# First part of an MLP: lower weight parts one K row behind the upper ones

## The chip, the cores and the metric

The kernel runs on one core of a Trainium2 chip. The metric is the device time of one execution in microseconds (us); the number given for a kernel is the median of several runs. TensorE (PE in the profile) multiplies, and its weight loads are shown as a row of their own (PEld). ScalarE (ACT), VectorE (DVE) and GpSimd (POOL) work on vectors, and SyncE (SP) issues the loads from memory.

## The reference

Two layers on 256 tokens of width 2048, everything in float32. Layer 0 mixes tokens with a convolution module, layer 1 with latent attention. Behind each of them comes an MLP with a hidden width of 8192:

```python
def sq_relu_mlp(h, w1, w2):
    return jnp.square(jax.nn.relu(h @ w1)) @ w2

for layer in range(DEPTH):
    h = rms_norm(x, norm_mixer_g[layer])
    x = x + (conv_module(h, ...) if layer % 2 == 0 else mla(h, ...))
    h = rms_norm(x, norm_mlp_g[layer])
    x = x + sq_relu_mlp(h, mlp_w1[layer], mlp_w2[layer])
return rms_norm(x, final_norm_g)
```

The change concerns the product `h @ w1`, in both layers.

## The kernel before

**Numbers in two parts.** A float32 value is split into an upper part (`hi`, rounded to the format float32r) and a lower part (`lo`, the remainder). A product of two such numbers is made of three: upper by upper, upper by lower, lower by upper. ScalarE makes the upper part of the weights (line 420) and VectorE the lower one (line 421).

**The up product.** The hidden width is cut into four parts (`q` = 0 to 3). Each part has eight pairs `p` of two tiles `b`, and a tile is 128 hidden columns for all 256 tokens. K, the width of 2048, is cut into 16 rows `k` of 128. The activations lie in `xt`: for each row `k` the upper parts of the 256 tokens and, beside them, the lower parts, so that `xhl(k)` is 512 columns wide and `xh(k)` its first 256. For each row TensorE loads the upper weight part and runs 512 columns (line 504), which gives two of the three products at once, and then loads the lower weight part and runs 256 columns (line 505). Both add into one PSUM tile of 512 columns. At the tile's end ScalarE copies it out (line 510), and VectorE adds its two halves (line 522).

**Units and chunks.** A tile's weights are a unit, one load of 1 MB. It is worked off in two chunks `h` of eight rows. A chunk's `prep` makes the two weight parts, in buffers of which there are six each (`WB`). Its `run` issues the matmuls. `stream` goes through the list of chunks and calls `prep` of up to five chunks ahead before `run` of the current one:

```python
while done[0] < min(n + (LOOK_UP if chunk.tight else WB), len(chunks)):
    ...
    prep()
...
chunk.run(parts[unit])
```

**Order.** The list begins with the 16 tiles of part 0, one directly after the other, and the first tile of part 1 follows them. From there on up tiles of part `q` + 1 stand singly between chunks of the down product of part `q`, which consist of 512-column matmuls (lines 195 to 197). Ahead of part 0, in both layers, stand the last transposes of the activations (line 251) that make `xt`; six of them lie inside its first tile. Each engine works off its instructions in the order in which they are written here, and semaphores keep the engines in step. A buffer is written again once the last reader of its earlier contents is through.

**What ties to the change.** The upper part of a chunk is last read by row 7 or 15 of line 504, the lower part by line 505 of the same row. The functions below are the ones that the change touches.

Of the kernel before, what the change touches and what calls it, by code (L numbers as in the profile page):

```python
# [20 lines left out]
KC = D // P  # L21
T = 2
S = T * P
# [59 lines left out]
def trunk_kernel(  # L83
# [26 lines left out]
    nc = tc.nc  # L110
# [28 lines left out]
    def nm(s):  # L139
        uid[0] += 1  # L140
        return f"{s}_{uid[0]}"


    def acc_tile():
        return psum["acc"].tile([P, NB], F32, tag="acc", name=nm("acc"))
# [41 lines left out]
    def rows(w, k0, nk, c0, n):  # L187

        return w[k0 * P : (k0 + nk) * P, c0 : c0 + n].rearrange(
            "(j p) n -> p j n", p=P  # L190
        )
# [128 lines left out]
    xh = lambda k: xhl(k)[:, :S]  # L320
# [95 lines left out]
    def hi_lo(n):  # L416
        return [wpool.tile([P, n, NB], F32R, tag=c, name=nm(c), bufs=WB) for c in ("hi", "lo")]

    def split_into(parts, src):
        nc.scalar.activation(parts[0], src, AF.Copy)  # L420
        nc.vector.tensor_tensor(parts[1], src, parts[0].bitcast(F32), op=ALU.subtract)  # L421
# [51 lines left out]
    def mlp(layer, ssq, next_gain, finish=None, before=None, last_w1=None):  # L473
# [5 lines left out]
        def u_tile():  # L479
            return first_tiles.pop("u", None) or mp.tile([P, 2, 2 * S], F32, tag="U", name=nm("U"), bufs=2)  # L480

        def f_tile():
            return first_tiles.pop("f", None) or mp.tile([P, 8, P], F32, tag="W", name=nm("W"), bufs=1)

        def up_units(hs, q, p, extra):

            sevens = SEVENS[layer][q]
            held = {}

            def up_unit(b):  # L490
                ps = []

                def chunk(h):
                    def prep(raw, parts):
                        parts[h] = [a.rearrange("p a (j n) -> p (a j) n", n=P) for a in hi_lo(2)]
                        split_into(parts[h], raw[:, 8 * h : 8 * h + 8, :])

                    def run(parts):
                        if not ps:
                            ps.append(acc_tile())  # L500
                        wh, wl = parts.pop(h)
                        for j in range(8):
                            k = 8 * h + j
                            nc.tensor.matmul(ps[0], wh[:, j, :], xhl(k), start=k == 0, stop=False)  # L504
                            nc.tensor.matmul(ps[0][:, :S], wl[:, j, :], xh(k), start=False, stop=k == KC - 1)  # L505

                    def out():
                        if b == 0:
                            held["u"] = u_tile()
                        nc.scalar.activation(held["u"][:, b, :], ps[0], AF.Copy)  # L510

                    if h == 0:
                        return Chunk(prep, run)
                    return Chunk(prep, run, [add, lambda: None, square, forms, part] + extra if b == 1 else [], now=out)

                unit = Unit(rows(w1, 0, KC, ((q * NPAIR + p) * 2 + b) * P, P), KC, [chunk(h) for h in range(2)])
                unit.last_read = 1
                return unit

            def add():  # L520
                v = held["u"][:, :, :S]
                nc.vector.tensor_tensor(v, v, held["u"][:, :, S:], op=ALU.add)

            def square():
                v = held["u"][:, :, :S]
                nc.scalar.activation(v, v, AF.Relu)
                if p in sevens:
                    held["f"] = f = f_tile()
                    nc.scalar.activation(f[:, 0:4, :].rearrange("p (b t) n -> p b (t n)", b=2), v, AF.Square)
                    held["src"], shape, tag, n = f[:, 1:8, :], [P, 7, P], "s", N_S  # L530
                else:
                    nc.scalar.activation(v, v, AF.Square)
                    held["src"], shape = v, [P, 2, S]
                    tag, n = ("s", N_S) if q == PARTS - 1 and p in LATE_G[layer] else ("g", N_G)
                held["hl"] = [mp.tile(shape, F32R, tag=tag + c, name=nm(tag + c), bufs=n) for c in "hl"]

            def forms():
                if p in sevens:
                    f = held["f"]
                    nc.vector.tensor_tensor(  # L540
                        f[:, 4:6, :], f[:, 0:1, :].broadcast_to([P, 2, P]), f[:, 1:3, :], op=ALU.subtract
                    )
                    nc.vector.tensor_tensor(f[:, 6, :], f[:, 1, :], f[:, 5, :], op=ALU.subtract)
                    nc.vector.tensor_tensor(f[:, 7, :], f[:, 3, :], f[:, 6, :], op=ALU.subtract)

            def part():
                hs[p] = held["hl"]
                split_into(hs[p], held["src"])

            return [up_unit(b) for b in range(2)]  # L550

        def down_units(hs, q, n2, held, final):
# [228 lines left out]
    with ExitStack() as cx:  # L781
# [40 lines left out]
        def conv_w(n, j):  # L822
            half = raws[n].shape[1] // 2
            hi, lo = wjs[n, j // half]
            return hi[:, j % half, :], lo[:, j % half, :]
# [174 lines left out]
        with tc.manual_schedule():  # L1000
# [143 lines left out]
            for m in range(NP):  # L1144
# [4 lines left out]
                for j in range(2):  # L1149
                    k = 2 * m + j  # L1150
                    wh, wl = conv_w(NU + m, j)
# [9 lines left out]
                t, i = divmod(m, NNB)  # L1161
# [68 lines left out]
    with ExitStack() as cx:  # L1230
# [73 lines left out]
        def w_at(key, j):  # L1304
            n = pieces[key]
            half = units[n][1][1] // 2
            hi, lo = parts[n, j // half]
            return hi[:, j % half, :], lo[:, j % half, :]
# [243 lines left out]
        with tc.manual_schedule():  # L1552
# [8 lines left out]
            ps = [[acc_tile() for _ in range(2)] for _ in range(T)]  # L1561
            for k in range(KC):
                u, j = divmod(k, 2)
# [6 lines left out]
                wh, wl = w_at(("kv", u), j)  # L1570
# [9 lines left out]
            ps = [acc_tile() for _ in range(T)]  # L1580
            for k in range(KC):
                u, j = divmod(k, 4)
# [3 lines left out]
                wh, wl = w_at(("q", u), j)  # L1586
# [176 lines left out]
```

## Time and profile before

| what | us |
|---|---|
| median of 3 runs | 1948.66 |
| lowest and highest run | 1948.26, 1950.67 |
| the profiled execution | 1952.0 |
| its span, first to last instruction | 1950.2 |
| TensorE busy in it | 1925.9 (99%) |

The granted TensorE clock was 0.999 of full speed over the span. Rows of the profile give a line of the kernel, an engine, an operation, the tile written and those read, the shape and a count; then busy time in us and the mean of one in ns. Rows of the timeline give the start and the duration in us. Matmuls overlap each other in these records, since each one's end is modelled with its way through the array: what one costs is the time from its start to the next start.

### The profile page before, as it was taken

The page shows a single profiled execution, that of the slowest core. Times are in us where ns is not written, and L with a number is a line of the kernel's source. Part 1 is how long each engine was busy: PE and PEld are TensorE (multiplying, and loading weights), DVE is VectorE, ACT ScalarE, POOL GpSimd, SP SyncE. Part 2 cuts the span into 40 slices and gives each one's busy share as a digit, 9 for nine tenths or more (in the row PEclk, how much of TensorE's full clock was granted, in tenths as well). Part 3 has the DMA queues.
Part 4 walks back from the last instruction along what each step waited for, and adds up shares of the span by engine and source line. Part 5 has one row for each costly group of instructions (what it writes and reads, how often), then busy time and mean ns, then how long its engine had stood idle before and what let it go on. Part 6 is the DMA issues. An engine that isn't in the chain of part 4 may idle for free.

```text
span 1950.2 us, 28404 instructions
## 1 busy us (share of the span) xinstructions
PE 1925.9 (99%) x10814; PEld 1681.3 (86%) x10814; DVE 1612.7 (83%) x2294; ACT 1196.1 (61%) x1695; POOL 223.8 (11%) x184
## 2 busy tenths in 40 slices
PE   7999999999999999999999999999999999999998
PEld 7999888888888888888899998888888888888886
DVE  5999866679998998898976665557999899889887
ACT  5556655666666666756566665566666566666644
POOL 5999300000000000000001410000000000000000
PEclk9999999999999999999999999999999999999999
DMA  8666356757666666766646445765666766666763
GB/s 237 181 180 188 131 193 183 207 154 216 192 206 197 202 194 202 216 185 213 200 149 181 118 148 175 213 174 169 196 196 205 206 205 195 191 207 197 226 205 108
DMA packets 407112, 367.61 MB, mean 188 GB/s; under 512 B 15416, under 2 KB 351936, under 8 KB 406720
## 3 DMA queue, kind: packets, MB, share of 16 engines
q1 hardware_dynamic: 405952, 363.63, 62.8%
q10 hardware_dynamic: 1024, 2.17, 0.3%
q8 instruction: 84, 1.38, 0.3%
q14 instruction: 52, 0.43, 0.1%
HBM read 363.68 MB, written 2.10 MB: 188 GB/s over the span
## 4 chain that ended last, share of the span: by engine, by line
PE 96%; ACT 1%; DVE 1%; DMA 1%; POOL 1%; issue 0%; DVEq 0%; ACTq 0%; POOLq 0%
PE acc L504 24%; PE acc L195 15%; PE acc L197 15%; PE acc L196 15%; PE acc L505 12%; PE acc L835 3%; PE acc L834 3%; PE acc L833 3%; PE acc L251 1%; PE sum L883 1%; PE acc L1531 0%; POOL lo L170 0%; DMA xs<-in_x 0%; ACT hi L169 0%; PE acc L1395 0%; PE acc L1396 0%
## 5 line engine op out<-in xcount | busy, mean ns | idle before, releaser
L504 PE MATMUL acc<-xt,hi 128*128 128x512 f32 x2048 | 718.6, 394 | 0.0
L421 DVE TENSOR_TENSOR lo<-raw,hi 128x1024 fp32r<-128x1024 f32 (+1 forms) x512 | 573.0, 1135 | 98.1 <-ACT hi L420 97.7
L505 PE MATMUL acc<-xt,lo 128*128 128x256 f32 x2048 | 574.4, 280 | 0.0
L420 ACT ACTIVATE hi<-raw 128x1024 fp32r<-128x1024 f32 (+1 forms) x512 | 491.0, 982 | 84.9 <-PE acc L196 68.5
L504 PEld LDWEIGHTS acc<-xt,hi 128*128 128x128 f32 x2048 | 384.4, 188 | 88.4
L505 PEld LDWEIGHTS acc<-xt,lo 128*128 128x128 f32 x2048 | 385.3, 188 | 3.7
L195 PE MATMUL acc<-hi,sh 128*128 128x512 f32 x814 | 319.4, 392 | 0.0
L197 PE MATMUL acc<-lo,sh 128*128 128x512 f32 x814 | 318.1, 391 | 0.0
L420 ACT ACTIVATE hi<-T 128x1024 fp32r<-128x1024 f32 x164 | 173.7, 1059 | 184.1 <-DVE T L696 124.8
L196 PE MATMUL acc<-hi,sl 128*128 128x512 f32 x686 | 267.3, 390 | 0.0
L421 DVE TENSOR_TENSOR lo<-T,hi 128x1024 fp32r<-128x1024 f32 x164 | 200.5, 1222 | 43.0 <-ACT hi L420 39.8
L169 ACT ACTIVATE hi<-raw 128x1024 fp32r<-128x1024 f32 (+2 forms) x184 | 179.9, 1005 | 44.9 <-PE acc L196 39.0
L170 DVE TENSOR_TENSOR lo<-raw,hi 128x1024 fp32r<-128x1024 f32 (+2 forms) x118 | 133.3, 1148 | 67.3 <-ACT hi L169 61.6
L510 ACT ACTIVATE U<-acc 128x512 f32<-128x512 f32 x128 | 76.1, 595 | 175.1 <-PE acc L505 175.0
L197 PEld LDWEIGHTS acc<-lo,sh 128*128 128x128 f32 x814 | 152.8, 188 | 33.6
L195 PEld LDWEIGHTS acc<-hi,sh 128*128 128x128 f32 x814 | 152.9, 188 | 32.4
L935 DVE SCALAR_TENSOR_TENSOR sum<-ub,w_dw,sum 128x256 f32<-128x256 f32 x400 | 162.7, 479 | 7.6 <-ACT sum L891 6.5
L170 POOL TENSOR_TENSOR lo<-raw,hi 128x1024 fp32r<-128x1024 f32 x66 | 157.7, 2412 | 24.4 <-ACT hi L169 24.4
L196 PEld LDWEIGHTS acc<-hi,sl 128*128 128x128 f32 x686 | 128.9, 188 | 24.0
L833 PE MATMUL acc<-xt,hi 128*128 128x256 f32 x512 | 145.3, 284 | 0.0
L834 PE MATMUL acc<-xt,hi 128*128 128x256 f32 x512 | 143.9, 281 | 0.4 <-DVE xt L208 0.4
L835 PE MATMUL acc<-xt,lo 128*128 128x256 f32 x512 | 144.0, 281 | 0.0
(265 smaller groups left out, 2756.4 us busy)
## 6 DMA issues: line engine op xcount, KB each, us to landing
raw<-in_mlp_w SPq DMA_DIRECT2D x256, 1024.0 KB, 6.1
raw<-in_conv_w_pw SPq DMA_DIRECT2D x64, 512.0 KB, 5.5
raw<-in_conv_w_pw SPq DMA_DIRECT2D x16, 1024.0 KB, 5.1
raw<-in_mla_w_o SPq DMA_DIRECT2D x16, 1024.0 KB, 5.8
raw<-in_mla_w_kv_up SPq DMA_DIRECT2D x8, 1024.0 KB, 5.6
raw<-in_mla_w_in SPq DMA_DIRECT2D x8, 576.0 KB, 3.8
raw<-in_mla_w_in SPq DMA_DIRECT2D x4, 1024.0 KB, 6.5
raw<-in_mla_w_q_up SPq DMA_DIRECT2D x16, 256.0 KB, 3.9
```

Source lines behind the costliest of these rows:

```text
L169: nc.scalar.activation(hi, raw[:, js, :], AF.Copy)
L170: eng.tensor_tensor(lo, raw[:, js, :], hi.bitcast(F32), op=ALU.subtract)
L195: nc.tensor.matmul(ps, sh, mh, start=start, stop=False)
L196: nc.tensor.matmul(ps, sl, mh, start=False, stop=False)
L197: nc.tensor.matmul(ps, sh, ml, start=False, stop=stop)
L420: nc.scalar.activation(parts[0], src, AF.Copy)
L421: nc.vector.tensor_tensor(parts[1], src, parts[0].bitcast(F32), op=ALU.subtract)
L504: nc.tensor.matmul(ps[0], wh[:, j, :], xhl(k), start=k == 0, stop=False)
L505: nc.tensor.matmul(ps[0][:, :S], wl[:, j, :], xh(k), start=False, stop=k == KC - 1)
L833: nc.tensor.matmul(o, wh[:, bs], xh(k), start=k == 0, stop=False)
L834: nc.tensor.matmul(o, wh[:, bs], xl(k), start=False, stop=False)
L835: nc.tensor.matmul(o, wl[:, bs], xh(k), start=False, stop=k == KC - 1)
```

## The change

In tiles of part 0 (`q == 0`) the matmul with the lower weight part of row `k` is issued after the matmul with the upper part of row `k` + 1. The sequence of a tile is hi0, hi1, lo0, hi2, lo1, and so on to hi15, lo14, lo15. The lower part of row 7, the last of the first chunk, is thus read in the second chunk's `run`, behind hi8. All other parts keep their order, since there `behind` is 0 and the list is emptied at once.

```diff
             def up_unit(b):
-                ps = []
+                ps, low, behind = [], [], int(q == 0)
...
                         for j in range(8):
                             k = 8 * h + j
                             nc.tensor.matmul(ps[0], wh[:, j, :], xhl(k), start=k == 0, stop=False)
-                            nc.tensor.matmul(ps[0][:, :S], wl[:, j, :], xh(k), start=False, stop=k == KC - 1)
+                            low.append((wl[:, j, :], k))
+                            while low and (len(low) > behind or k == KC - 1):
+                                a, i = low.pop(0)
+                                nc.tensor.matmul(ps[0][:, :S], a, xh(i), start=False, stop=i == KC - 1)
```

## The prediction

> **What bounds the kernel now.** I read the page first: the busy line, the chain and the two groups of the lines that change.
>
> ```profile
> span 1950.2 us, 28404 instructions
> ...
> PE 1925.9 (99%) x10814; PEld 1681.3 (86%) x10814; DVE 1612.7 (83%) x2294; ACT 1196.1 (61%) x1695; POOL 223.8 (11%) x184
> ...
> PE 96%; ACT 1%; DVE 1%; DMA 1%; POOL 1%; issue 0%; DVEq 0%; ACTq 0%; POOLq 0%
> ...
> L504 PE MATMUL acc<-xt,hi 128*128 128x512 f32 x2048 | 718.6, 394 | 0.0
> ...
> L505 PE MATMUL acc<-xt,lo 128*128 128x256 f32 x2048 | 574.4, 280 | 0.0
> ```
>
> TensorE ends nearly every step of the chain, so only what moves its matmuls together or apart can move the end. The durations 394 and 280 ns are not what a matmul costs: matmuls overlap, and the cost is the distance from one start to the next. The page cannot show that, so I went on to stages. An up tile is 32 matmuls, 16 pairs of a 512-column one on the upper weight part (L504) and a 256-column one on the lower part (L505). I asked for busy time by stretch, over 15 tiles of the first part in each layer and over two tiles further on:
>
> ```profile
> 325.02:409.82 84.80, 84.80 (x483) 73.64 (x482) 58.45 (x82) 52.89 (x70) 0.00 (x0) 1.00 0.64 178
> 1267.05:1351.85 84.80, 84.80 (x482) 73.64 (x481) 53.32 (x61) 51.81 (x66) 0.00 (x0) 1.00 0.63 177
> 420.25:425.80 5.55, 5.55 (x33) 4.87 (x32) 5.04 (x13) 3.05 (x4) 0.00 (x0) 1.00 0.63 174
> 867.20:872.75 5.55, 5.55 (x33) 4.87 (x32) 5.31 (x7) 2.85 (x3) 0.00 (x0) 1.00 0.44 170
> ```
>
> The first number behind the stretch is its length, the pair of brackets behind 84.80 the matmuls (480 belong to the 15 tiles, the others reach in at the edges), and 1.00 is the granted clock. A tile of the first part takes 84.80 / 15 = 5.653 us, or 353.3 ns a pair. A tile of a later part takes 5.55 us, or 346.9 ns a pair. The instructions, the operands' shapes, the clock and the DMA share are the same, and TensorE waits for nobody in either. This difference of 0.10 us a tile is what the change can act on. The timeline of TensorE alone shows where it sits:
>
> ```profile
> 325.01 0.40 PE L504 MATMUL acc<-xt,hi 128*128 128x512 f32 x1
> 325.25 0.28 PE L505 MATMUL acc<-xt,lo 128*128 128x256 f32 x1
> 325.38 0.39 PE L504 MATMUL acc<-xt,hi 128*128 128x512 f32 x1
> 325.61 0.28 PE L505 MATMUL acc<-xt,lo 128*128 128x256 f32 x1
> 325.72 0.40 PE L504 MATMUL acc<-xt,hi 128*128 128x512 f32 x1
> ```
>
> Every second 512-column matmul lasts 0.40 instead of 0.39 us, and the next start comes 0.24 instead of 0.23 us later. Two pairs take 0.71 us (2 x 353.3 ns). In a later tile:
>
> ```profile
> 419.57 0.39 PE L195 MATMUL acc<-hi,sh 128*128 128x512 f32 x1
> ...
> 420.25 0.40 PE L504 MATMUL acc<-xt,hi 128*128 128x512 f32 x1
> 420.49 0.28 PE L505 MATMUL acc<-xt,lo 128*128 128x256 f32 x1
> 420.60 0.39 PE L504 MATMUL acc<-xt,hi 128*128 128x512 f32 x1
> 420.83 0.28 PE L505 MATMUL acc<-xt,lo 128*128 128x256 f32 x1
> ...
> 421.30 0.39 PE L504 MATMUL acc<-xt,hi 128*128 128x512 f32 x1
> ```
>
> This tile comes straight after 512-column matmuls. Its first one lasts 0.40 us, and from then on all pairs are short (420.60 to 421.30 are two pairs in 0.70 us). So the same stream of pairs has two rhythms, each of which keeps itself up: the slow one through 15 tiles with nothing to break it, the fast one for all the 16 pairs of a tile that was entered out of a run of 512-column matmuls. The first part's stream is entered differently, out of transposes:
>
> ```profile
> 319.30 0.82 PE L251 MATMUL acc<-ident,xs 128*128 128x128 f32 x6
> ```
>
> **The change part by part.** It gives tiles of the first part the order hi0, hi1, lo0, hi2, lo1 ... hi15, lo14, lo15. No instruction is added or taken away. Per tile there is one step 512 to 512 and one step 256 to 256 more, and one step 512 to 256 and one step 256 to 512 fewer. There are 16 such tiles a layer, 32 in all.
>
> Removed: if each tile now falls into the fast rhythm because it begins with two 512-column matmuls, a tile gains 5.653 - 5.55 = 0.103 us. That holds for 15 tiles a layer. The layer's first tile has the six transposes in it and is entered out of them whatever the order, and the tile right after the 16 (the first of the second part, unchanged, directly behind two 256-column matmuls) may be in either rhythm: I take half, 0.05 us, for each. That is 15 x 0.103 + 0.10 = 1.65 us a layer, 3.3 us in both.
>
> Added: the steps themselves. What a 512-column step costs in a settled run is (420.25 - 419.57) / 3 = 0.227 us, against 0.23 inside a pair. For 256 after 256 the nearest rows are the convolution's stage, 10 steps in 1.19 us:
>
> ```profile
> 99.72 0.28 PE L834 MATMUL acc<-xt,hi 128*128 128x256 f32 x1
> ...
> 100.91 0.28 PE L835 MATMUL acc<-xt,lo 128*128 128x256 f32 x1
> ```
>
> That is 0.119 us, against 346.9 - 230 = 117 ns for the 256-column step of a fast pair. So the steps as such cost 0.00 us. What may cost something is settling. Where pairs turn into 512-column matmuls, the first six take longer than six settled ones:
>
> ```profile
> 425.80 0.40 PE L195 MATMUL acc<-hi,sh 128*128 128x512 f32 x1
> ...
> 427.19 0.39 PE L195 MATMUL acc<-hi,sh 128*128 128x512 f32 x1
> ```
>
> 1.39 us against 6 x 0.227 = 1.36: 0.03 us a turn. The new tile has one step of this kind instead of six, so between 0 and the whole 0.03 us, 0 to 0.96 us over 32 tiles. I take 0.01 us (two of six steps), 0.3 us in all, since it is nearer to one step than to six.
>
> Waits: the lower part of row 7 is now read one 512-column step into the next half tile, so its buffer comes free some 0.35 us later (0.12 + 0.23). VectorE's write into that buffer comes behind ScalarE's write of the matching upper part, whose own buffer is freed at the same place as before.
>
> ```profile
> L420 ACT ACTIVATE hi<-raw 128x1024 fp32r<-128x1024 f32 (+1 forms) x30 | 31.1, 1039 | 1.9 <-PE acc L504 1.9
> ```
>
> ```profile
> DVE lo L421 <- ACT hi L420: 21.0, 24, 2.3
> ...
> PEld acc L251 <- DVE xs L336: 0.5, 1, 0.5
> ```
>
> The first row is a group of the 15 tiles' stretch, the others are waits over the whole first part of layer 0. ScalarE needs 1.04 us a write, and VectorE waits for exactly that (the second row), so 0.35 us lies beneath it and costs nothing. Were the cover gone, VectorE would start 0.35 us late, and behind it in its queue stand the additions of the U tiles. TensorE would still not notice: it has only one wait in this stage, the 0.5 us of the last row, at its beginning, and the parts are made up to five halves (14 us) ahead. The copy out of PSUM still waits for the tile's last 256-column matmul as before. No DMA is moved.
>
> Sum: -3.3 + 0.3 = -3.0 us. The profiled execution took 1952.0 us with a span of 1950.2, that is 3.3 us above the median of the runs, 1948.66. No step of the sum depends on that difference, so I take it off the median: 1945.7 us (the span would be 1947.2).
>
> **A rule that speaks against it.** The Trainium skill, "TensorE: Matmul & The Clock Gate", section "Step-by-step: what each phase is for", says that the weights of the next matmul come through a read port of their own, and that "Loading the next tile's weights doesn't steal SBUF read bandwidth from the running matmul." Its section "Back-to-back issue gap" makes the distance a function of the column count alone, an estimate of 215.8 + 109.2 = 325 ns for a pair. By these two a tile's order cannot matter and the change is worth nothing. It would leave the time where it is, which is the first rival below. The trace disagrees on the second section: the same pair takes 353.3 ns in one place and 346.9 in another.
>
> **The rivals.** The slow rhythm stays. Then only settling is left: 0 to +0.96 us, 1948.7 to 1949.6 us. For it speaks that a run of 512-column matmuls is no cure by itself; in the second product of the convolution module such a run stays slow:
>
> ```profile
> 255.79 0.39 PE L195 MATMUL acc<-hi,sh 128*128 128x512 f32 x1
> ...
> 257.85 0.39 PE L195 MATMUL acc<-hi,sh 128*128 128x512 f32 x1
> ```
>
> These are nine steps in 2.06 us, 0.229 us each and not 0.227. Also, one step between two 512-column matmuls may be too short to reset what long runs reset. Against it speaks that both later tiles shown are fast from their second pair on, with nothing else ahead of them than such steps. To this rival belongs a half success, in which the fast rhythm holds for a few pairs of a tile and falls back: with 4 of 16 pairs fast it gives 4/16 x 3.3 = 0.8 us, 1947.9.
>
> The slower side: the new order puts another weight load beside each matmul (lo of the row before beside a 512-column one), and every pair, not every second, gets the long form. A long pair is 2 x 353.3 - 346.9 = 359.7 ns, 6.4 ns above today's mean; 512 pairs give 3.3 us, and with the full settling 0.96 us it is +4.2 us, 1952.9. It decides the sign if more than every second pair is long. Nothing in the profile shows two long pairs in a row, so I hold it unlikely.
>
> That the change doesn't do what it says can be left out: only the order of one engine's queue is edited.
>
> **How the numbers follow.** A measurement of this kernel tells about 0.2%, 3.9 us, from no change. Forecast 0.64, slow rhythm stays or comes back 0.28, every pair long 0.08. The forecast's own range is 1945.2 (both doubtful tiles gained, 17 x 0.103 x 2 = 3.5, no settling) to 1946.7 (settling in full, neither doubtful tile: 3.1 - 0.96 = 2.1). The lowest of the three runs lies 0.4 us under the median, and the same again may come in on the other kernel: low 1944.4. Up, the range takes in the first rival with full settling: 1949.6. Over 0.2% faster needs the far end and the scatter: 0.20 of the forecast's 0.64. The rest of it and the first rival are within 0.2%: 0.44 + 0.28 = 0.72. Slower: 0.08.
>
> **What would show it.** Right: 15 tiles of the first part in some 83.3 us instead of 84.80 in both layers, 512-column matmuls of 0.39 us after each tile's first two, and nothing else moved. Wrong: alternate 0.40 and 0.39 us as now (first rival), 0.40 throughout (second), or TensorE waiting for VectorE's lo at the middle of a tile, which would overturn the argument on the buffer.

## The result: 3 us longer, because the first part is now slow in every execution

The changed kernel takes 1951.8 us (median of 22 runs, 1951.53 to 1952.76), the kernel before 1948.64 us in the same comparison (22 runs, 1948.26 to 1951.95). The ratio is 1.0013, with a 95% interval from 1.0007 to 1.0019. That is slower by less than 0.2%, with an interval clear of no change, and outside the predicted range, which ended at 1949.6.

The times of before are not one heap. Of its 22 runs 13 lie between 1948.26 and 1948.66, six between 1949.97 and 1950.9 and three between 1951.88 and 1951.95: three groups, 1.7 us apart. The runs of the changed kernel form one group, around the last of these three. The profiled execution of before, at 1952.0 us, came from the last group.

The page of the changed kernel shows almost nothing of this:

```profile
span 1949.8 us, 28404 instructions
...
PE 1926.0 (99%) x10814; PEld 1681.7 (86%) x10814; DVE 1611.2 (83%) x2294; ACT 1194.2 (61%) x1695; POOL 223.5 (11%) x184
...
L504 PE MATMUL acc<-xt,hi 128*128 128x512 f32 x2048 | 716.0, 394 | 0.0
...
L508 PE MATMUL acc<-xt,lo 128*128 128x256 f32 x2048 | 569.1, 280 | 0.0
```

The span is 0.4 us shorter than that of the execution shown of before, and yet the kernel is slower: a reader of the two pages alone would call it a small gain. Busy times by stretch say more. These are the 15 tiles behind the first one, in both layers of the changed kernel (line 508 is the old line 505):

```profile
324.93:409.66 84.73, 84.73 (x482) 73.75 (x481) 59.50 (x89) 52.22 (x70) 0.00 (x0) 1.00 0.64 178
1266.79:1351.52 84.73, 84.73 (x482) 73.72 (x481) 53.03 (x61) 51.17 (x66) 0.00 (x0) 1.00 0.62 177
```

84.73 us against 84.80 in the profile of before: 5.649 us a tile, the slow rhythm. The timeline of TensorE at the end of the first tile shows how it gets there:

```profile
324.39 0.39 PE L504 MATMUL acc<-xt,hi 128*128 128x512 f32 x1
324.62 0.40 PE L508 MATMUL acc<-xt,lo 128*128 128x256 f32 x2
324.86 0.63 PE L504 MATMUL acc<-xt,hi 128*128 128x512 f32 x2
325.32 0.28 PE L508 MATMUL acc<-xt,lo 128*128 128x256 f32 x1
...
326.49 0.39 PE L504 MATMUL acc<-xt,hi 128*128 128x512 f32 x1
326.72 0.28 PE L508 MATMUL acc<-xt,lo 128*128 128x256 f32 x1
326.84 0.40 PE L504 MATMUL acc<-xt,hi 128*128 128x512 f32 x1
327.08 0.28 PE L508 MATMUL acc<-xt,lo 128*128 128x256 f32 x1
327.20 0.39 PE L504 MATMUL acc<-xt,hi 128*128 128x512 f32 x1
```

The rows with x2 are the double steps that the change makes: lo14 and lo15, then hi0 and hi1 of the next tile. Up to there the first tile's 512-column matmuls last 0.39 us each. A few pairs later 0.39 and 0.40 alternate, and the tiles stay at 5.65 us to the end of the part.

### The profile page after: what moved, and what is told of

The parts are those of the page before. It is cut to its first block, busy times and chain, and to the rows that moved or that the text cites. A ratio compares the mean times of both kernels' runs of the same rounds, so it can differ in the third digit from the quotient of the medians.

```text
span 1949.8 us, 28404 instructions
## 1 busy us (share of the span) xinstructions
PE 1926.0 (99%) x10814; PEld 1681.7 (86%) x10814; DVE 1611.2 (83%) x2294; ACT 1194.2 (61%) x1695; POOL 223.5 (11%) x184
## 4 chain that ended last, share of the span: by engine, by line
PE 96%; DVE 1%; ACT 1%; DMA 1%; issue 0%; POOL 0%; DVEq 0%; ACTq 0%
PE acc L504 24%; PE acc L195 15%; PE acc L197 15%; PE acc L196 15%; PE acc L508 12%; PE acc L838 3%; PE acc L837 3%; PE acc L836 3%; PE acc L251 1%; PE sum L886 1%; PE acc L1534 0%; DMA xs<-in_x 0%; PE acc L1398 0%; PE acc L1399 0%; PE acc L1400 0%
```

## The experiments

**The kernel before once more.** No edit. My theory A after the result: each layer's first part falls into one of two rhythms at its entry, anew in every execution. The profile of before had caught both layers slow, most of its runs had not, and the change makes all of them slow. Rival B: the first part is always slow before the change, and the change loses its 3 us elsewhere.

> The kernel before, unchanged. Theory A (each layer's first part falls into the slow or the fast rhythm at its entry, anew in every execution, and the profile shown of before caught both layers slow): the times fall into groups about 1.7 us apart, near 1948.5, 1950.2 and 1951.9, and in a profile each layer's 15 tiles take either 83.3 or 84.8 us, with the execution's time higher by 1.5 to 1.7 us for each slow layer. Theory B (the first part is always slow before the change, and the change loses its 3 us elsewhere): the profile shows 84.8 us in both layers whatever its own time is.

Measured: 11 runs from 1948.37 to 1952.29 us (ratio 1.0003, interval 0.9994 to 1.0012), with 28 runs of before beside them that cover the same range. The profiled execution, at 1950.92 us, has one layer of each kind:

```profile
324.93:408.13 83.20, 83.20 (x482) 73.12 (x482) 58.08 (x83) 52.69 (x70) 0.00 (x0) 1.00 0.65 183
1265.21:1350.01 84.80, 84.80 (x482) 73.64 (x482) 53.03 (x61) 51.79 (x66) 0.00 (x0) 1.00 0.62 178
```

The first row is layer 0, 83.20 / 15 = 5.547 us a tile; the second is layer 1, 5.653 us. It is the same program on the same inputs. B falls: the first part is not always slow. With 1.6 us a layer in 15 tiles and 0.1 us in the tile behind them, no, one or two slow layers make three groups 1.7 us apart. Executions with one and with two slow layers were profiled; that the lowest group has none is inferred from its times.

How often an execution falls into the lowest group is not fixed. It was 13 of 22 in the first comparison, but 11 of 28, 5 of 31 and 4 of 20 in the three comparisons that the experiments come from (by their times, and by the span where a time lies between two groups). There the kernel before has its median at 1950.2 us and not at 1948.64. A ratio below is taken against that, so a kernel at 1952 us loses as much as the changed one, although its ratio may be lower.

**The new order in one tile alone.** Two kernels, in which `behind` is 1 only for the first tile of the part, or only for the ninth:

```diff
-                ps, low, behind = [], [], int(q == 0)
+                ps, low, behind = [], [], int(q == 0 and p == MADE[layer][0][0] and b == 0)   # first
+                ps, low, behind = [], [], int(q == 0 and p == MADE[layer][0][4] and b == 0)   # ninth
```

> Only the first tile of each layer's first part has the new order, the 15 others the old one. Theory A with the end of the tile as the culprit (two 256-column matmuls in a row, then 512 columns, throw a fast stream into the slow rhythm, which then keeps itself): first tile fast, tiles 1 to 16 slow in every execution, 1951.8 us like the changed kernel. Rival (the new order must be repeated in every tile to do harm): tiles 2 and on fast, 1948.5 us. Theory B: no change from before, with before's scatter.

> Only the ninth of the 16 tiles has the new order. Theory A with a single disturbance being enough: tiles 1 to 7 fast or slow as the entry had it, tiles 9 to 16 slow in every execution, so times of 1950.1 us and more (8 tiles of 0.10 us in two layers, 1.6 us above 1948.5), up to 1951.9. Rival (one disturbance heals, or throws either way): times as before or, in executions that entered slowly, lower.

With the first tile alone the kernel takes 1952.03 us (10 runs, 1951.87 to 1952.14; ratio 1.0013, 1.0004 to 1.0022): as much as the whole change, and again without groups. Its 15 other tiles, which have the old order, are slow in both layers, and the timeline shows the turn at the first tile's end:

```profile
324.92:409.72 84.80, 84.80 (x482) 73.69 (x481) 59.39 (x89) 52.67 (x70) 0.00 (x0) 1.00 0.64 180
1266.90:1351.70 84.80, 84.80 (x482) 73.69 (x481) 53.11 (x61) 51.80 (x66) 0.00 (x0) 1.00 0.63 178
```

```profile
324.68 0.39 PE L504 MATMUL acc<-xt,hi 128*128 128x512 f32 x1
324.91 0.40 PE L508 MATMUL acc<-xt,lo 128*128 128x256 f32 x2
325.14 0.39 PE L504 MATMUL acc<-xt,hi 128*128 128x512 f32 x1
325.37 0.28 PE L508 MATMUL acc<-xt,lo 128*128 128x256 f32 x1
325.49 0.40 PE L504 MATMUL acc<-xt,hi 128*128 128x512 f32 x1
```

Here only 256 columns follow 256 columns (the x2 row); the next tile begins with a single 512-column matmul, and its second one already lasts 0.40 us. The first tile's own double step of 512 columns stands ahead of the six transposes, and the pairs behind these are fast.

With the ninth tile alone it takes 1950.47 us (10 runs, 1950.24 to 1951.04; ratio 1.0006, 0.9996 to 1.0015). The seven tiles behind the first, and the seven behind the ninth:

```profile
324.97:363.80 38.83, 38.83 (x226) 34.13 (x225) 27.35 (x44) 24.57 (x34) 0.00 (x0) 1.00 0.66 179
...
369.44:409.00 39.56, 39.56 (x226) 34.36 (x225) 27.34 (x34) 24.57 (x31) 0.00 (x0) 1.00 0.61 179
```

38.83 / 7 = 5.547 us ahead of it, 39.56 / 7 = 5.651 us behind it. And the beginning of the ninth tile:

```profile
363.38 0.39 PE L504 MATMUL acc<-xt,hi 128*128 128x512 f32 x1
363.61 0.28 PE L508 MATMUL acc<-xt,lo 128*128 128x256 f32 x1
363.72 0.63 PE L504 MATMUL acc<-xt,hi 128*128 128x512 f32 x2
364.19 0.28 PE L508 MATMUL acc<-xt,lo 128*128 128x256 f32 x1
364.30 0.39 PE L504 MATMUL acc<-xt,hi 128*128 128x512 f32 x1
364.53 0.28 PE L508 MATMUL acc<-xt,lo 128*128 128x256 f32 x1
364.65 0.40 PE L504 MATMUL acc<-xt,hi 128*128 128x512 f32 x1
```

Here 512 columns follow 512 (the x2 row) in the middle of a fast stream, long before the tile's closing pair of 256, and two pairs later the slow rhythm is there. So either double step is enough to throw a fast stream into the slow rhythm, and in the first tile alone it costs as much as in all 16. What I had not expected is that all ten runs of the ninth-tile kernel lie in one narrow group. They fit an entry that is fast each time (1948.5 + 16 x 0.10 = 1950.1), although the tiles ahead of the ninth are those of before. The entry is thus not mere chance in every kernel; what sets it stays open.

**No double steps within the part.** The lower part is still one row behind, but row 15's is carried over into the next tile, so that 512 and 256 columns alternate all through the part:

```diff
...
+                            carry.append((ps[0], wl[:, j, :], k, None if end_of_part else ended))
+                            while carry and (len(carry) > int(q == 0) or (end_of_part and k == KC - 1)):
+                                o, a, i, fn = carry.pop(0)
+                                nc.tensor.matmul(o[:, :S], a, xh(i), start=False, stop=i == KC - 1)
...
```

> Lower parts one row behind the upper ones as in the changed kernel, but carried over the tile's end: row 15's lower part comes behind row 0's upper part of the next tile, so that 512 and 256 columns alternate through the whole part, with one double step at its beginning and one at its end. Theory A: no double step disturbs the stream, so the tiles keep the rhythm of the entry: 1948.5 us where it is fast, and never the changed kernel's constant 1951.8. Rival (the harm comes from which weight load lies beside which matmul, lo of the row before beside a 512-column one): slow as in the changed kernel, 1951.8 us in every execution.

Measured: 1955.23 us (5 runs; ratio 1.0032, 1.002 to 1.0044), slower than either theory said. In the profile both layers were slow from their first tile on (the row is layer 0), and the kernel also lost something that has nothing to do with the rhythm. The waits of TensorE and of its weight loads in the down product behind the first part of layer 0:

```profile
325.15:409.84 84.69, 84.69 (x482) 73.53 (x481) 58.30 (x88) 52.07 (x69) 0.00 (x0) 1.00 0.65 179
```

```profile
PE acc L197 <- DVE lo L421: 0.5, 1, 0.5
```

```profile
PEld acc L197 <- DVE lo L421: 1.0, 1, 1.0
PEld acc L195 <- ACT hi L420: 0.6, 1, 0.6
```

The down product waits for its upper and lower weight parts, 0.6 and 1.0 us by the two weight-load rows, and the matmuls behind that place start 1.3 us later than in the profile of before; layer 1 loses 1.3 us in the same way. That is 2.6 of the 3.3 us above 1951.9; the rest was not followed up. By the code the reason is that a tile's copy and everything behind it are issued half a tile later, which no run shows by itself. The experiment shows only that a stream can be slow from its entry with no double step in it behind the transposes, as before's can. It doesn't decide on the rival, since the entry was not fast.

**Runs of 512 columns as a cure.** In the later parts every tile comes out of a run of 512-column matmuls and is fast. Theory A held that such a run sets the fast rhythm. Two kernels test it: the first tile's second half issues its eight lower parts first and its upper ones last, and so does the ninth tile's after eight tiles of the changed order (for which `behind` is 1 where `p in MADE[layer][0][:4]`).

```diff
+                        if q == 0 and p == MADE[layer][0][0] and b == 0 and h == 1:   # [4] for the ninth tile
+                            for j in range(8):
+                                nc.tensor.matmul(ps[0][:, :S], wl[:, j, :], xh(8 + j), start=False, stop=False)
+                            for j in range(8):
+                                nc.tensor.matmul(ps[0], wh[:, j, :], xhl(8 + j), start=False, stop=j == 7)
+                            return
```

> Order of before, but the second half of each layer's first tile issues its eight lower parts first and then its eight upper parts, so that the second tile is entered out of a run of 512-column matmuls, as the tiles of the later parts are. Theory A (a run of 512-column matmuls sets the fast rhythm, and a stream without double steps keeps it): tiles 1 to 16 take 5.55 us in every execution and both layers, 1948.5 us without the groups at 1950.2 and 1951.9. Rival (what a stream of pairs falls into is chance at any entry): three groups as before.

> The changed order in tiles 0 to 7 of each first part, then one tile of the old order whose second half issues its lower parts first and its upper parts last, then seven tiles of the old order. Theory A (a run of 512-column matmuls ends the slow rhythm as well): tiles 1 to 7 slow, 5.65 us, tiles 9 to 16 fast, 5.55 us, in both layers and every execution, 1950.1 to 1950.3 us. Rival (once slow, the stream stays slow until the down product): 1951.9 us.

Measured: 1952.01 us (11 runs, 1951.89 to 1952.58; ratio 1.0009, 1.0000 to 1.0018) and 1951.95 us (10 runs; ratio 1.0009, 1.0000 to 1.0019). Both are slow in every execution, so this half of theory A falls. The first kernel's tiles behind the run, and the second kernel's tiles 9 to 15:

```profile
324.98:409.78 84.80, 84.80 (x481) 73.82 (x480) 58.67 (x83) 52.88 (x70) 0.00 (x0) 1.00 0.64 178
```

```profile
370.20:409.78 39.58, 39.58 (x226) 34.48 (x225) 27.45 (x34) 24.56 (x31) 0.00 (x0) 1.00 0.61 179
```

The timeline of the first one shows that such a run is itself not what it is in the down product:

```profile
323.13 2.02 PE L506 MATMUL acc<-xt,hi 128*128 128x512 f32 x8
325.00 0.40 PE L510 MATMUL acc<-xt,hi 128*128 128x512 f32 x1
```

From the run's first start at 323.13 to the next matmul behind it at 325.00 are eight steps, 0.234 us each. In the down product a step of 512 columns after 512 takes 0.227 us, once six steps are past; here the run's last two steps are as long as its first ones. The widths and the granted clock are the same; the operands differ. Here the moving columns are the activations `xt` and the loaded weights come from the weight buffers; there it is the weight buffers that move.

**All upper parts of a half, then all lower ones**, in the first part and in all parts:

```diff
+                        if q == 0:   # or: True
+                            for j in range(8):
+                                k = 8 * h + j
+                                nc.tensor.matmul(ps[0], wh[:, j, :], xhl(k), start=k == 0, stop=False)
+                            for j in range(8):
+                                k = 8 * h + j
+                                nc.tensor.matmul(ps[0][:, :S], wl[:, j, :], xh(k), start=False, stop=k == KC - 1)
+                            return
```

> In all tiles of the first part each half issues its eight upper parts, then its eight lower parts. Theory A leaves no stream of pairs that could be slow: a settled run takes 0.227 us a 512-column and 0.117 us a 256-column step, 5.50 us a tile, 1.4 us below the fast case over 32 tiles, 1947.1 us; with 0.03 us of settling in each half 1949.0. One group of times. Rival (runs have a slow form too, as in the convolution's second product, 0.229 and 0.119 us): 5.57 us a tile, 1949.2 us and more.

> The same order in all 128 tiles of the two up products. If settled runs cost 5.50 us a tile, it gains 0.05 us on each of 128 tiles, some 5.5 us below the fast case: 1943 us; with settling of 0.03 us in each half 1950.7. Rival (slow form of runs): 0.02 us a tile more than pairs, 1951 us and more.

Measured: 1951.18 us (10 runs; ratio 1.0004, 0.9995 to 1.0013) and 1955.47 us (8 runs; ratio 1.0026, 1.0016 to 1.0036). The rows of the first part, in the first kernel and in the second:

```profile
325.00:409.40 84.40, 84.40 (x483) 73.70 (x482) 59.20 (x89) 51.78 (x70) 0.00 (x0) 1.00 0.65 180
```

```profile
324.98:409.38 84.40, 84.40 (x482) 73.71 (x481) 59.16 (x89) 51.78 (x70) 0.00 (x0) 1.00 0.65 180
```

84.40 / 15 = 5.627 us a tile in both: 0.08 us more than fast pairs, 0.03 less than slow ones. With steps of 0.227 and 0.117 us it would be 5.50, so the step of the down product isn't to be had in the up product as `xt` lies here. In all parts the order costs 4.3 us more, over the 96 tiles of the later parts; the two later tiles shown of before were fast, 5.55 us.

**Moving the activations by 64 and 128 bytes.** The runs of the last two experiments led to theory C: what a 512-column step costs, and with it the slow rhythm, depends on where the moving columns lie against the weights that are loaded beside them. `xt` lies behind a small pad on the right side of the memory, so its place can be moved alone with what shares its pool:

```diff
-PAD_RIGHT = 48
+PAD_RIGHT = 32   # 64 bytes a partition; 16: 128 bytes
```

Each move was made in the kernel before and in the changed one.

> The kernel before, with the activations xt (and what shares their pool) moved by 16 floats, 64 bytes, in each partition; nothing else. Theory C (what a 512-column step costs, and with it the slow rhythm, depends on where the moving columns and the next weights lie against each other): the first part's tiles take another time than 5.547 or 5.653 us, or only one of the two; stages that read xt change, the down product stays at 0.227 us a step. Theory A (the rhythm comes from the order of matmul widths alone): two rhythms as before, 5.547 and 5.653 us, three groups of times.

> The changed kernel with the same move by 64 bytes. Theory C: the double step at a tile's beginning costs something else than now, and the tiles need not be slow: within 0.5 us of the moved kernel before it. Theory A: 5.65 us a tile from the second tile on, as in the changed kernel, 3.2 us above the moved kernel's fastest executions.

> As the first of these, moved by 32 floats, 128 bytes. Theory C: a third time for the tiles, or one of the others. Theory A: two rhythms as before.

> The changed kernel moved by 128 bytes. Theory C: differs from the moved kernel before it by another amount than 3 us. Theory A: slow from the second tile on, 5.65 us.

Moved by 64 bytes, the order of before takes 1947.74 us (10 runs, 1946.15 to 1948.38; ratio 0.9986, 0.9976 to 0.9995), the changed one 1947.8 us (ratio 0.9988, 0.9979 to 0.9997). The 15 tiles of both layers with the old order, then with the new one in layer 0:

```profile
325.29:408.48 83.19, 83.19 (x481) 73.76 (x480) 58.30 (x84) 52.67 (x70) 0.00 (x0) 1.00 0.65 183
1264.86:1348.06 83.20, 83.20 (x481) 73.76 (x480) 52.88 (x61) 51.46 (x66) 0.00 (x0) 1.00 0.63 181
```

```profile
325.25:408.75 83.50, 83.50 (x482) 73.62 (x481) 59.25 (x89) 52.30 (x70) 0.00 (x0) 1.00 0.65 181
```

The old order is fast in both layers. The new one costs 0.30 us in 15 tiles, 0.02 us for each pair of double steps, and not 0.10: a double step disturbs the stream, but the slow rhythm doesn't come. Moved by 128 bytes it is 1958.28 us (4 runs; ratio 1.0042, 1.0027 to 1.0057) and 1958.08 us (5 runs; ratio 1.0040, 1.0026 to 1.0054), and the tiles of the first part take a third time, with the old order and with the new:

```profile
327.09:411.09 84.00, 84.00 (x482) 73.28 (x481) 58.43 (x83) 52.77 (x70) 0.00 (x0) 1.00 0.65 180
```

```profile
327.05:411.16 84.11, 84.11 (x482) 73.31 (x482) 59.33 (x89) 52.21 (x70) 0.00 (x0) 1.00 0.64 180
```

5.600 and 5.607 us. Theory C also says that other stages that read `xt` change and the down product does not. So it is. By 64 bytes, ten 256-column steps of the convolution's first product take 1.16 us (the prediction's rows: 1.19):

```profile
99.74 0.28 PE L833 MATMUL acc<-xt,hi 128*128 128x256 f32 x1
...
100.90 0.28 PE L834 MATMUL acc<-xt,hi 128*128 128x256 f32 x1
```

By 128 bytes, the tile that took 5.55 us in the first down product takes 5.61, while six steps of the down product ahead of it stay at 1.36 us, 0.227 each:

```profile
420.13 0.39 PE L195 MATMUL acc<-hi,sh 128*128 128x512 f32 x1
...
421.49 0.40 PE L504 MATMUL acc<-xt,hi 128*128 128x512 f32 x1
```

```profile
421.49:427.10 5.61, 5.61 (x33) 4.89 (x32) 5.10 (x13) 3.05 (x4) 0.00 (x0) 1.00 0.63 172
```

The time of 1958 us has its source in such stages: along the trace it is lost in the convolution's first product and in the up tiles of all parts. So the place of `xt`, and of what shares its pool, sets what these steps cost. With the order unchanged, no slow tile is seen at 64 bytes, and at 128 the tiles take another time; of the three places only the first one loses 3 us by the change. Whether the place itself counts or the distance from the weights, as the theory has it, these moves don't separate. The move by 64 bytes beats both kernels of this case. Most of that is the slow layers: the lowest executions of before beside it took 1948.3 us, 0.6 more than its median. The times at 64 bytes fall into two groups of their own (1946.15 to 1946.86 and 1947.73 to 1948.38), which I did not follow up; the profiled execution, with both layers fast, is of the upper one.

## Why the prediction was wrong

The prediction saw the two rhythms, and that they are what the change acts on. Three of its steps failed. The time came out 6.1 us above the 1945.7 forecast: 3.3 us from the first step below, 3.0 us because the gain did not come, which rests on the other two, less 0.2 us by which the changed kernel lies under the profiled execution of before.

"No step of the sum depends on that difference, so I take it off the median". This step put the sum, and the bounds of the range with it, on the wrong base. The difference between the profiled execution and the median, 3.3 us, was exactly the sum that I had just worked out for two slow layers. I had both numbers and did not put them side by side. In the median's executions there was nothing left to save: 13 of 22 runs lay in the group without a slow layer. The first rival, "the slow rhythm stays", had the same fault. Its place was not 1948.7 but that of the profiled execution, and the changed kernel, at 1951.8, is it: 1948.5 us, and for each layer 15 x (5.649 - 5.547) = 1.53 us and 0.10 in the tile behind, 3.3 us in all.

"If each tile now falls into the fast rhythm because it begins with two 512-column matmuls": the mechanism of the forecast, and the opposite happened. In the ninth-tile kernel a double 512-column step ended a fast stream within two pairs, and with the first tile alone a double 256-column step did. I took the entry out of a long run of the down product, where other operands move, for a property of the widths. The profile had a warning that I quoted and set aside: the convolution's second product, whose run stays slow.

"The steps as such cost 0.00 us." The 0.227 us of a 512-column step came from the down product. In the up product's own runs it is 0.234 us. As a cost this was small (0.007 x 32 = 0.2 us), and so was the 0.01 us of settling a tile, against 0.02 us for both double steps where nothing else comes with them (the move by 64 bytes). What it meant, that a step's cost hangs on its operands, was the heart of the case.

Two smaller slips changed nothing: 2.1 us off 1948.66 is 1946.5 and not 1946.7, and of the two later tiles shown one had a DMA share of 0.44, not the same as the first part's 0.64. The layers of the second profile of before, 0.65 fast and 0.62 slow, show that this share does not make the rhythm.

What held: TensorE's order was all that moved, and no wait came with the buffer that is freed later. In the first part of layer 0 the changed kernel's TensorE waits only at the beginning, as before's did:

```profile
PEld acc L251 <- DVE xs L336: 0.7, 2, 0.5
```

The slower rival, every pair long, did not come; the sign came out on its side by another mechanism, the loss of executions that had been fast. The sign that the prediction set for this rival, 0.40 us throughout, would have misled: in the kernel whose first tile ends with a run of upper parts, all 512-column rows behind it show 0.40 us in layer 0, and a tile takes the same 5.653 us (84.80 / 15) as with 0.39 and 0.40 in turn.

On the rule that spoke against the change: the order does matter here, and so does a move by 64 bytes. The Trainium skill, "TensorE: Matmul & The Clock Gate", section "Step-by-step: what each phase is for", has weight loads and moving columns on ports of their own, from which the prediction took it that a tile's order cannot matter. In these runs the same pairs took 5.547, 5.600 or 5.653 us a tile at a granted clock of 1.00, so the measurement decides against that conclusion for this kernel. The formula that the prediction takes from the section "Back-to-back issue gap" is given there for a matmul by itself; for a stream the section lets the weight loads count too. Why the place of the operands matters inside the chip, no run here shows.

## What to carry to other kernels

If one profile's time differs from the median of the runs, look for the sum under discussion in that difference first: the profile may show a case that the executions around the median don't have. When a stream of matmuls has two rhythms, count how often each occurs before pricing a way out, and test the operands' placement with a pad of 64 bytes before the order of issue. The cost of a step is taken from rows with the same operands, not only with the same widths.

## What the runs showed of the hardware

A stream of weight loads and matmuls can run for 85 us at 353.3 or at 346.7 ns a pair (84.80 and 83.20 us for 240 pairs), at the same granted clock of 1.00, and which of the two it is can differ between two layers of one execution. One doubled step, in a part of 512 matmuls, turned the fast form into the slow one (38.83 us for seven tiles ahead of it, 39.56 behind); the reverse was not seen within the part. With the moving operand 64 bytes away only the fast form was seen, in two layers of one profile (83.19 and 83.20 us).
